# A two-block transformer kernel: order inside the attention slots, where softmax steps end, two-block dilated slots, start and end of the program

## Chip, cores and metric

The kernel runs on one core of a Trainium2 chip. The metric is device time in microseconds (us), the median of several runs. Engines are called as the profile calls them: PE (TensorE matmul; PEld its weight loads), DVE (VectorE), ACT (ScalarE), POOL (GpSimd), SP (SyncE, which issues DMAs).

## What is computed

A residual stream of 512 tokens with 1024 channels goes through a forgetting attention ("fox", 16 heads of 64), a gated linear layer, a dilated attention (8 heads, three groups of keys), a second gated layer, and then a second block: a short convolution beside an attention with a compressed, a selected and a windowed branch, and a feed-forward layer. Cut to the parts that the change touches:

```python
# fox: every head, causal, with decay c
s = q @ k.T * 64**-0.5 + c[t] - c[s]; s = where(causal, s, -inf)
o = softmax(s) @ v;  out = (o * silu(z)) @ w_out
# dilated: 8 heads, groups g = 0, 1, 2 (window 128, 512, 2048; stride 1, 4, 16)
o_g, lse_g = window_attention(q_g, k_g, v_g, slopes_g)
o = sum_g softmax(lse)_g * o_g;  out = (o * silu(z)) @ w_out
# second block, 8 heads in 2 groups
o_c = softmax(q @ k_cmp.T) @ v_cmp      # 31 compressed keys
out = gate_c * o_c + gate_s * o_sel + gate_w * o_win
```

## The kernel before

Activations lie with channels on the partitions and the 512 tokens in the free dimension. Every big product is exact to nearly fp32 by three matmuls: weights and activations are split into a high part (`hi`, written by ACT) and a rest (`lo`, subtracted by DVE), and `mm3` (lines 144 to 146) runs hi·hi, hi·lo and lo·hi with 512 columns each. `Weights` brings the weights in units of 128x1024 through SP's queue (`wraw`), makes `whi` on ACT (line 74) and `wlo` on DVE (line 85); `pump` first finishes the last `wlo`, then starts new DMAs, then the next `whi`. `plan` is the list of units in the order of their use.

The program is written out by hand; each engine runs its instructions strictly in the order in which the Python code issues them. Projections are cut into chunks of four k-steps (12 matmuls of `mm3`): `t_unit` makes two chunks of one unit and lets its last chunk evacuate the accumulator (PSUM tag `acc`, 3 banks). `weave(chunks, slots)` deals the attention's slots evenly behind the chunks.

**Fox slots.** A head has three parts (`BLOCKS`: query block 3; blocks 2 and 0; block 1), so 48 steps for 16 heads. Slot j holds `soft_end` for what is open, then `t_step(j-4)` (transposes of the probabilities into a bank `t`, 2 banks, and their copies to `pt` by ACT), then `s_step(j)`, then in every sixth slot `pv_step` (probabilities times values, one pair of heads). `s_step` takes a bank `s` (2 banks), runs the scores (lines 678, 679), adds the mask by a matmul of a bf16 identity with the mask (line 542), and starts the softmax: `soft` (line 624, DVE) adds the decay, writes `pr` and the row's extreme `st`, then ACT takes the exponential with its sum (line 628). `soft_end` finishes all open softmax steps on DVE: reciprocals of the sums (line 637), then the scaling of `pr` (lines 640, 642). It is called at the head of every slot and, in a chunk, just ahead of the evacuation. One pair of heads is a cycle of six chunks (q, k, z) and six slots; cycles 1 to 6 are alike.

**Dilated slots.** A head has 4 steps of one query block each. `s_step(h, i)` runs one score matmul of the full array (line 814) and eight with 32 columns of the array each (line 818); three DVE operations, a reduction and the exponential follow. Slots lag by 3 steps; four slots go with the 14 chunks of a head (its z first, then q and k of the next head).

**Second block.** Its 48 steps work like fox's (`mwin` as mask on DVE, no mask matmul) and are woven with the convolution's and the gates' chunks; `c_scores`, `c_soft`, `ct_step` hold the compressed branch, whose values `vc2` (64x128) are multiplied by two matmuls of 32 rows and 64 columns of the array for every pair of heads (line 1281).

Of the kernel before, what the change touches and what calls it, by code (L numbers as in the profile page):

```python
# [26 lines left out]
class Weights:  # L27
# [20 lines left out]
    def start_halves(self, n, half):  # L48

        c = slice(half * S, half * S + S)  # L50
        for i in range(n):
            if half == 0:
                self.raw[i] = self.pool.tile([P, D], F32, name="wraw", tag="wraw", bufs=self.raw_bufs)
            self.nc.sync.dma_start(self.raw[i][:, c], self.units[i][1][:, c])
        self.n_dma = n

    def prep_half(self, i, half):
# [4 lines left out]
        self.nc.scalar.activation(hi[:, c], self.raw[i][:, c], AF.Copy)  # L62
# [65 lines left out]
class Net:  # L128
# [19 lines left out]
    def t_unit(self, tag, pair, kts, evac, m=P, tag_ps="acc"):  # L148
# [7 lines left out]
        for u, lst in enumerate(kts):  # L156
            for c0 in range(0, len(lst), 4):
                sub = lst[c0 : c0 + 4]

                def chunk(u=u, sub=sub, c0=c0, first=(c0 == 0), pos=pos):  # L160
                    if pos == 0:
                        st["acc"] = self.bank(tag_ps)
                    if first:
                        st["w"] = self.w.pop(tag)
                    self.w.pump()
# [17 lines left out]
    def k_outer(self, tags, evacs, pair):  # L183
# [3 lines left out]
        def chunk(k):  # L187
            if k == 0:
                st["w"] = [self.w.pop(t) for t in tags]
                st["a"] = [self.acc() for _ in tags]  # L190
            self.w.pump()
# [35 lines left out]
    def n_chunk(self, tag, lhs, pair, evac, banks=("acc", "acc", "acc", "s")):  # L227
# [3 lines left out]
        for u in range(4):  # L231
            for half in range(2):

                def chunk(u=u, half=half):
                    if half == 0:
                        if u == 0:
                            st["a"] = [self.bank(x) for x in banks]
                        st["w"] = self.w.pop(tag)
                    if u < 3:
# [105 lines left out]
    def plan(self):  # L345
# [15 lines left out]
        for h in range(8):  # L361
# [4 lines left out]
            add("dz", "dil_z", [h])  # L366
            if h < 7:
                for g in range(3):
                    add("dq", "dil_q", [8 * g + h + 1]); add("dk", "dil_k", [8 * g + h + 1])
        add("do", "dil_o", range(8))  # L370
# [17 lines left out]
    def run(self):  # L388
# [16 lines left out]
        nc.sync.dma_start(self.gains[:, 0:5, :], t["gains"])  # L405
# [31 lines left out]
    def fox(self):  # L437
# [6 lines left out]
        warm = at.tile([P, D], BF16, name="cb", tag="cb", bufs=3)[:, :S]  # L444
        nc.vector.memset(warm, 0.0)
        nc.scalar.activation(warm[:, 0:1], warm[:, 0:1], AF.Copy)
        idle = self.bank("o")
        for _ in range(9):
            nc.tensor.matmul(idle, warm[:, :P], warm, start=True, stop=True)
        x_load = lambda k: nc.sync.dma_start(xs[:, k, :], self.rows(t["xT"], k))  # L450
        x_load(0)
        self.w.start_halves(3, 0)
        x_load(1)
        x_load(2)
        self.w.start_halves(3, 1)
        for k in range(3, KT):
            x_load(k)
        feed = lambda k: self.feed(A, k, xs[:, k, :], self.gains[:, 0, k : k + 1])
        feed(0)
        for i in range(3):  # L460
# [70 lines left out]
        def s_step(j):  # L531
            h, part = divmod(j, 3)
            p = h // 2
            if part == 0 and h + 2 < 16:
                load_c(h + 2)
            sp = self.bank("s")
            pr = at.tile([P, S], F32, name="pr", tag="pr", bufs=6)
            blocks = self.BLOCKS[part]
            for qb, c0 in blocks:
                n = (qb + 1) * P  # L540
                self.scores(sp[:, c0 : c0 + n], qs[p], ks[p], h % 2, qb, False)
                nc.tensor.matmul(sp[:, c0 + n - P : c0 + n], identb, maskb, start=False, stop=True, skip_group_check=True)
            for qb, c0 in blocks:
# [13 lines left out]
        def slot(j):  # L557
            self.soft_end()
            if 0 <= j - LAG < 48:
                self.t_step(at, pts, probs, j - LAG)  # L560
            if j < 48:
                s_step(j)
            u = j - LAG - 7
            if u >= 0 and u % 6 == 0 and u // 6 < 8:
                pv_step(u // 6)
# [107 lines left out]
    def scores(self, out, qs, ks, j, qb, stop):  # L673
# [4 lines left out]
        self.nc.tensor.matmul(out, qs[j][:, c], hi[:, 0:n], start=True, stop=False, skip_group_check=True)  # L678
        self.nc.tensor.matmul(out, qs[j][:, c], lo[:, 0:n], start=False, stop=stop, skip_group_check=True)  # L679

    def t_step(self, at, pts, probs, j):
# [6 lines left out]
        for kb in ((0,), (1, 3), (2,))[part]:  # L688
# [78 lines left out]
    def dil(self):  # L767
# [9 lines left out]
        def ev_q(h, g):  # L777
            def f(a):
                q = qs[h, g] = at.tile([P, S], F32, name="dqk", tag="dqk", bufs=10)
# [4 lines left out]
        def ev_k(h, g):  # L784
            def f(a):
                k = ks[h, g] = at.tile([P, S], F32, name="dqk", tag="dqk", bufs=10)
# [22 lines left out]
        def s_step(h, i):  # L809
            sp = self.bank("s")  # L810
            pr = at.tile([P, S], F32, name="pr", tag="pr", bufs=4)
            q, k = [qs[h, g] for g in range(3)], [ks[h, g] for g in range(3)]
            lo = 0 if i else P
# [776 lines left out]
```

## Time and profile before

| | us |
|---|---|
| median of 3 runs | 1729.88 |
| lowest, highest | 1728.58, 1729.96 |
| profiled execution, device time | 1729.0 |
| its span, first to last instruction | 1727.2 |
| PE busy | 1714.4 (99%) |
| DVE busy | 966.0 (56%) |
| ACT busy | 672.2 (39%) |
| POOL busy | 111.0 (6%) |

Busy time of PE is from a start to a modelled end, and successive matmuls overlap, so PE at 99% says that it nearly always has one in flight, not that none is late. How far one start lies behind the one before is read from the timeline. Times of rows count from the span's start. The granted TensorE clock is full in the whole span.

### The profile page before, as it was taken

How to read it: one execution, taken by the hardware profiler on the slowest of the kernel's cores; microseconds unless marked ns; L12 is line 12 of the kernel's file. 1: busy time of each engine (PE TensorE's matmuls, PEld its weight loads, DVE VectorE, ACT ScalarE, POOL GpSimd, SP SyncE). 2: the span in 40 equal slices, each digit the busy share in tenths (PEclk: the TensorE clock that was granted, in tenths of full speed). 3: DMA queues.
4: the chain of work that ended last, by engine and by line, in shares of the span. 5: the costliest groups of instructions: out<-in, count | busy, mean ns of one | idle time of the engine just before them, and what ended most of it. 6: DMA issues, size and time to landing. Idle time of an engine off the chain costs nothing.

```text
span 1727.2 us, 21619 instructions
## 1 busy us (share of the span) xinstructions
PE 1714.4 (99%) x8512; PEld 1398.8 (81%) x8512; DVE 966.0 (56%) x1692; ACT 672.2 (39%) x1146; POOL 111.0 (6%) x88
## 2 busy tenths in 40 slices
PE   8999999999999999999999999999999999999999
PEld 6777777888978888978878887777788888888887
DVE  5577774453354543354555687776554675566432
ACT  6466663522222222222235545555432333333320
POOL 2000000100000000000000421000000222111000
PEclk9999999999999999999999999999999999999999
DMA  5322224323221222221223332112243432223321
GB/s 187 130 85 87 90 74 138 125 96 133 86 86 61 86 73 98 86 86 63 85 98 121 134 124 85 58 53 88 83 142 112 163 119 98 89 97 104 142 96 61
DMA packets 57349, 173.74 MB, mean 101 GB/s; under 512 B 7440, under 2 KB 7952, under 8 KB 57248
## 3 DMA queue, kind: packets, MB, share of 16 engines
q1 hardware_dynamic: 57248, 172.36, 29.0%
q8 instruction: 67, 1.10, 0.3%
q14 instruction: 34, 0.28, 0.1%
HBM read 161.82 MB, written 10.52 MB: 100 GB/s over the span
## 4 chain that ended last, share of the span: by engine, by line
PE 96%; DVE 2%; ACT 1%; DMA 0%; issue 0%; SPq 0%; ACTq 0%; DVEq 0%
PE acc L144 22%; PE acc L145 21%; PE acc L146 21%; PE acc L248 3%; PE acc L250 3%; PE acc L249 3%; PE o L700 2%; PE t L692 2%; PE s L144 1%; PE s L145 1%; PE s L146 1%; PE s L249 1%; PE s L248 1%; PE s L679 1%; PE s L250 1%; PE s L678 1%
## 5 line engine op out<-in xcount | busy, mean ns | idle before, releaser
L85 DVE TENSOR_TENSOR wlo<-wraw,whi 128x1024 fp32r<-128x1024 f32 x267 | 347.9, 1309 | 140.1 <-ACT whi L74 140.0
L74 ACT ACTIVATE whi<-wraw 128x1024 fp32r<-128x1024 f32 x267 | 279.0, 1050 | 152.7 <-PE acc L145 64.4
L628 ACT ACTIVATE pr<-pr,st 128x512 f32<-128x512 f32 (+3 forms) x160 | 93.6, 586 | 153.4 <-DVE st L825 84.1
L291 POOL TENSOR_TENSOR nacc<-nacc,sq 128x512 f32<-128x512 f32 x35 | 47.9, 1377 | 1186.3 <-ACT sq L290 1185.9
L781 DVE TENSOR_TENSOR dqk<-acc,nacc 128x512 f32<-128x512 f32 x24 | 26.1, 1102 | 61.6 <-PE s L814 57.5
L695 ACT ACTIVATE pt<-t 128x512 f32<-128x512 f32 (+3 forms) x128 | 51.0, 424 | 21.1 <-PE t L692 20.6
L1425 ACT ACTIVATE fy<-fcv,fcw 128x512 f32<-128x512 f32 x22 | 17.9, 816 | 100.0 <-DVE fcv L1420 100.0
L1438 POOL TENSOR_TENSOR act<-fs,fu 128x512 f32<-128x512 f32 x22 | 43.2, 1966 | 191.0 <-DVE fu L1437 174.0
L692 PE MATMUL t<-ident,pr 128*128 128x128 f32 x320 | 50.8, 273 | 2.0 <-ACT pt L695 1.1
L692 PEld LDWEIGHTS t<-ident,pr 128*128 128x128 f32 x320 | 40.0, 140 | 14.0 <-DVE pr L640 1.4
L144 PE MATMUL acc<-a0h,whi 128*128 128x512 f32 x112 | 47.3, 422 | 2.0 <-ACT whi L62 1.4
L824 DVE SCALAR_TENSOR_TENSOR pr<-dist,s 128x128 f32<-128x128 f32 (+1 forms) x96 | 24.9, 314 | 42.2 <-PE s L818 42.2
L144 PE MATMUL acc<-b4h,whi 128*128 128x512 f32 x113 | 45.6, 404 | 0.0
L637 DVE RECIPROCAL st<-st 128x1 f32<-128x1 f32 x160 | 23.8, 158 | 38.6 <-ACT pr L628 38.6
L144 PE MATMUL acc<-b7h,whi 128*128 128x512 f32 x113 | 44.2, 391 | 0.0
L144 PE MATMUL acc<-b5h,whi 128*128 128x512 f32 x113 | 44.2, 391 | 0.0
L146 PE MATMUL acc<-a0h,wlo 128*128 128x512 f32 x112 | 44.1, 394 | 0.0
L144 PE MATMUL acc<-b6h,whi 128*128 128x512 f32 x113 | 44.1, 390 | 0.0
L146 PE MATMUL acc<-b7h,wlo 128*128 128x512 f32 x113 | 44.1, 390 | 0.0
L145 PE MATMUL acc<-b4l,whi 128*128 128x512 f32 x113 | 44.0, 390 | 0.0
L146 PE MATMUL acc<-b6h,wlo 128*128 128x512 f32 x113 | 44.0, 390 | 0.0
L146 PE MATMUL acc<-b4h,wlo 128*128 128x512 f32 x113 | 44.0, 389 | 0.0
(1108 smaller groups left out, 4680.7 us busy)
## 6 DMA issues: line engine op xcount, KB each, us to landing
wraw<-in_dil_q SPq DMA_DIRECT2D x24, 512.0 KB, 3.2
wraw<-in_dil_k SPq DMA_DIRECT2D x24, 512.0 KB, 3.2
wraw<-in_dil_v SPq DMA_DIRECT2D x24, 512.0 KB, 3.3
wraw<-in_f_g SPq DMA_DIRECT2D x22, 512.0 KB, 3.5
wraw<-in_f_u SPq DMA_DIRECT2D x22, 512.0 KB, 3.5
wraw<-in_f_o SPq DMA_DIRECT2D x22, 512.0 KB, 3.5
wraw<-in_gate SPq DMA_DIRECT2D x16, 512.0 KB, 3.3
wraw<-in_b_gm SPq DMA_DIRECT2D x16, 512.0 KB, 3.5
```

What stands on the lines that cost most here:

```text
L74: nc.scalar.activation(hi, t, AF.Copy)
L85: self.nc.vector.tensor_tensor(lo, t, hi.bitcast(F32), ALU.subtract)
L144: mm(acc, wh, xh, start=start, stop=False)
L145: mm(acc, wh, xl, start=False, stop=False)
L146: mm(acc, wl, xh, start=False, stop=stop)
L248: self.nc.tensor.matmul(a, sh, mh, start=(k == 0), stop=False)
L249: self.nc.tensor.matmul(a, sh, ml, start=False, stop=False)
L250: self.nc.tensor.matmul(a, sl, mh, start=False, stop=(k == KT - 1))
L291: nc.gpsimd.tensor_tensor(self.nacc[i], self.nacc[i], sq, ALU.add)
L628: self.nc.scalar.activation(pr, pr, AF.Exp, scale=-1.0, bias=st[:, 0:1], accum_out=st[:, 1:2])
L692: nc.tensor.transpose(tp[:, c : c + P], pr[:, c0 + kb * P : c0 + (kb + 1) * P], self.ident)
L695: nc.scalar.activation(pts[h][:, self.KOFF[kb] : self.KOFF[kb] + b - a], tp[:, a:b], AF.Copy)
```

## The change

- In every chunk of a projection (`t_unit`, `k_outer`, `n_chunk`, `t_two`) a call of `soft_end` stands directly ahead of `self.w.pump()`.
- A fox slot is ordered `pv_step`, `t_step`, mask matmuls, scores, softmax. In the second block `pv_step` moves to the front and the compressed branch's steps go ahead of `s_step`.
- `t_step` transposes key block 2 first, then 1 and 3, then 0.
- A dilated slot takes two query blocks: their full-array scores, then all their 32-column scores, then both softmax starts; it lags by two slots, and two slots go with a head's chunks. z is computed behind q and k of the next head, and z of heads 6 and 7 together in the last phase.
- `vc2` becomes block diagonal (64x2x128), and one matmul takes the place of two.
- At the start, the first halves of the first three weight units are issued from ACT's queue, `gains` follow the pool's set-up, and the first `whi` half is made by DVE. At the end, the last output tile is added and stored in two halves.

```diff
@@ -54 +54 @@
-            self.nc.sync.dma_start(self.raw[i][:, c], self.units[i][1][:, c])
+            (self.nc.sync if half else self.nc.scalar).dma_start(self.raw[i][:, c], self.units[i][1][:, c])
@@ -62 +62,4 @@
-        self.nc.scalar.activation(hi[:, c], self.raw[i][:, c], AF.Copy)
+        if i + half:
+            self.nc.scalar.activation(hi[:, c], self.raw[i][:, c], AF.Copy)
+        else:
+            self.nc.vector.tensor_copy(hi[:, c], self.raw[i][:, c])
@@ -164,0 +168 @@
+                    self.soft_end()
@@ -190,0 +195 @@
+            self.soft_end()
@@ -238,0 +244 @@
+                    self.soft_end()
@@ -366 +371,0 @@
-            add("dz", "dil_z", [h])
@@ -369,0 +375,2 @@
+            if h != 6:
+                add("dz", "dil_z", [h] if h < 6 else [6, 7])
@@ -405 +411,0 @@
-        nc.sync.dma_start(self.gains[:, 0:5, :], t["gains"])
@@ -444,6 +449,0 @@
-        warm = at.tile([P, D], BF16, name="cb", tag="cb", bufs=3)[:, :S]
-        nc.vector.memset(warm, 0.0)
-        nc.scalar.activation(warm[:, 0:1], warm[:, 0:1], AF.Copy)
-        idle = self.bank("o")
-        for _ in range(9):
-            nc.tensor.matmul(idle, warm[:, :P], warm, start=True, stop=True)
@@ -450,0 +451 @@
+        nc.sync.dma_start(self.gains[:, 0:5, :], t["gains"])
@@ -454,0 +456,6 @@
+        warm = at.tile([P, D], BF16, name="cb", tag="cb", bufs=3)[:, :S]
+        nc.vector.memset(warm, 0.0)
+        nc.scalar.activation(self.sel[:, 0:1], self.ones, AF.Copy)
+        idle = self.bank("o")
+        for _ in range(9):
+            nc.tensor.matmul(idle, warm[:, :P], warm, start=True, stop=True)
@@ -458,0 +466 @@
+        self.w.prep_half(0, 0)
@@ -460 +468 @@
-        for i in range(3):
+        for i in range(1, 3):
@@ -536,2 +543,0 @@
-            sp = self.bank("s")
-            pr = at.tile([P, S], F32, name="pr", tag="pr", bufs=6)
@@ -539 +545,2 @@
-            for qb, c0 in blocks:
+            sp = self.bank("s")
+            for i, (qb, c0) in enumerate(blocks):
@@ -541,3 +548,13 @@
-                self.scores(sp[:, c0 : c0 + n], qs[p], ks[p], h % 2, qb, False)
-                nc.tensor.matmul(sp[:, c0 + n - P : c0 + n], identb, maskb, start=False, stop=True, skip_group_check=True)
-            for qb, c0 in blocks:
+                nc.tensor.matmul(sp[:, c0 + n - P : c0 + n], identb, maskb, start=(i == 0), stop=False, skip_group_check=True)
+            return lambda: s_scores(h, part, sp)
+
+        def s_scores(h, part, sp):
+            p = h // 2
+            for qb, c0 in self.BLOCKS[part]:
+                n = (qb + 1) * P
+                self.scores(sp[:, c0 : c0 + n], qs[p], ks[p], h % 2, qb, True, False)
+            return lambda: s_soft(h, part, sp)
+
+        def s_soft(h, part, sp):
+            pr = at.tile([P, S], F32, name="pr", tag="pr", bufs=6)
+            for qb, c0 in self.BLOCKS[part]:
@@ -559,4 +575,0 @@
-            if 0 <= j - LAG < 48:
-                self.t_step(at, pts, probs, j - LAG)
-            if j < 48:
-                s_step(j)
@@ -565,0 +579,4 @@
+            if 0 <= j - LAG < 48:
+                self.t_step(at, pts, probs, j - LAG)
+            if j < 48:
+                s_step(j)()()
@@ -673 +690 @@
-    def scores(self, out, qs, ks, j, qb, stop):
+    def scores(self, out, qs, ks, j, qb, stop, start=True):
@@ -678 +695 @@
-        self.nc.tensor.matmul(out, qs[j][:, c], hi[:, 0:n], start=True, stop=False, skip_group_check=True)
+        self.nc.tensor.matmul(out, qs[j][:, c], hi[:, 0:n], start=start, stop=False, skip_group_check=True)
@@ -688 +705 @@
-        for kb in ((0,), (1, 3), (2,))[part]:
+        for kb in ((2,), (1, 3), (0,))[part]:
@@ -779 +796 @@
-                q = qs[h, g] = at.tile([P, S], F32, name="dqk", tag="dqk", bufs=10)
+                q = qs[h, g] = at.tile([P, S], F32, name="dqk", tag="dqk", bufs=12)
@@ -786 +803 @@
-                k = ks[h, g] = at.tile([P, S], F32, name="dqk", tag="dqk", bufs=10)
+                k = ks[h, g] = at.tile([P, S], F32, name="dqk", tag="dqk", bufs=12)
@@ -809,3 +826,2 @@
-        def s_step(h, i):
-            sp = self.bank("s")
-            pr = at.tile([P, S], F32, name="pr", tag="pr", bufs=4)
+        def s_step(h, i0):
+
@@ -812,0 +829,16 @@
+            sps = []
+            for i in (i0, i0 + 1):
+                sps.append(self.bank("s"))
+                lo = 0 if i else P
+                nc.tensor.matmul(sps[-1][:, lo:256], q[0][:, i * P : (i + 1) * P], k[0][:, (i - 1) * P + lo : (i + 1) * P],
+                                 start=True, stop=True, skip_group_check=True)
+            for i, sp in zip((i0, i0 + 1), sps):
+                for g in (1, 2):
+                    for r in range(4):
+                        nc.tensor.matmul(sp[32 * r : 32 * r + 32, 128 + g * P : 256 + g * P],
+                                         q[g][:, i * P + 32 * r : i * P + 32 * r + 32], k[g][:, r * P : (r + 1) * P],
+                                         start=True, stop=True, skip_group_check=True)
+            for i, sp in zip((i0, i0 + 1), sps):
+                s_soft(h, i, sp)
+
+        def s_soft(h, i, sp):
@@ -814,7 +846 @@
-            nc.tensor.matmul(sp[:, lo:256], q[0][:, i * P : (i + 1) * P], k[0][:, (i - 1) * P + lo : (i + 1) * P],
-                             start=True, stop=True, skip_group_check=True)
-            for g in (1, 2):
-                for r in range(4):
-                    nc.tensor.matmul(sp[32 * r : 32 * r + 32, 128 + g * P : 256 + g * P],
-                                     q[g][:, i * P + 32 * r : i * P + 32 * r + 32], k[g][:, r * P : (r + 1) * P],
-                                     start=True, stop=True, skip_group_check=True)
+            pr = at.tile([P, S], F32, name="pr", tag="pr", bufs=6)
@@ -857,2 +882,0 @@
-        LAG = 3
-
@@ -863,7 +887,8 @@
-                u = j - LAG
-                if u >= 4 and u % 4 == 0:
-                    pv_step(h0 + u // 4 - 1)
-                if 0 <= u < 16:
-                    t_step(h0 + u // 4, u % 4)
-                if j < 16:
-                    s_step(h0 + j // 4, j % 4)
+                u = j - 2
+                if u >= 2 and u % 2 == 0:
+                    pv_step(h0 + u // 2 - 1)
+                if 0 <= u < 8:
+                    for i in range(2):
+                        t_step(h0 + u // 2, u % 2 * 2 + i)
+                if j < 8:
+                    s_step(h0 + j // 2, j % 2 * 2)
@@ -871 +896 @@
-            return [lambda j=j: slot(j) for j in range(16 + LAG + 1)]
+            return [lambda j=j: slot(j) for j in range(11)]
@@ -898 +923 @@
-            ch = T("dz", ev_z(h))
+            ch = []
@@ -902,5 +927,6 @@
-            n = 4 if h < 7 else 2
-            if h == 7:
-                run(ch)
-            weave(ch if h < 7 else [], todo[:n])
-            todo = todo[n:]
+            if h < 6:
+                ch += T("dz", ev_z(h))
+            elif h == 7:
+                ch = T("dz", ev_z(6)) + T("dz", ev_z(7))
+            weave(ch, todo[:2])
+            todo = todo[2:]
@@ -964 +990,2 @@
-        vc2 = at.tile([64, P], F32, name="vc2")
+        vc2 = at.tile([64, 2, P], F32, name="vc2")
+        nc.gpsimd.memset(vc2, 0.0)
@@ -1133 +1160,4 @@
-            nc.scalar.activation(vc2, p[:, :P], AF.Copy)
+            src = p[:, :P].rearrange("p (g d) -> p g d", g=2)
+            for j in range(2):
+                r = slice(32 * j, 32 * j + 32)
+                nc.scalar.activation(vc2[r, :, 64 * j : 64 * j + 64], src[r], AF.Copy)
@@ -1280,3 +1310 @@
-                for jj in range(2):
-                    nc.tensor.matmul(ob[p][64 * jj : 64 * jj + 64, :], vc2[32 * jj : 32 * jj + 32, g * 64 : g * 64 + 64],
-                                     ptc[p][32 * jj : 32 * jj + 32, :], start=True, stop=False, skip_group_check=True)
+                nc.tensor.matmul(ob[p], vc2[:, g, :], ptc[p], start=True, stop=False, skip_group_check=True)
@@ -1291,0 +1320,3 @@
+            u = j - LAG - 7
+            if u >= 0 and u % 6 == 0 and u // 6 < 8:
+                pv_step(u // 6)
@@ -1296,0 +1328,5 @@
+            if j in (1, 19):
+                c_scores(j // 19)
+            for g in range(2):
+                if 0 <= j - 3 - 18 * g < 4:
+                    c_soft(g, j - 3 - 18 * g)
@@ -1299,8 +1334,0 @@
-                if j in (1, 19):
-                    c_scores(j // 19)
-                for g in range(2):
-                    if 0 <= j - 3 - 18 * g < 4:
-                        c_soft(g, j - 3 - 18 * g)
-            u -= 7
-            if u >= 0 and u % 6 == 0 and u // 6 < 8:
-                pv_step(u // 6)
@@ -1384,0 +1413 @@
+            self.soft_end()
@@ -1473,2 +1502,3 @@
-            v.tensor_tensor(res[n], res[n], acc[n], ALU.add)
-            nc.sync.dma_start(self.rows(t["out"], n), res[n])
+            for c in (slice(0, 256), slice(256, S)) if n == KT - 1 else (slice(0, S),):
+                v.tensor_tensor(res[n][:, c], res[n][:, c], acc[n][:, c], ALU.add)
+                nc.sync.dma_start(self.rows(t["out"], n)[:, c], res[n][:, c])
```

The order on DVE in cycle 1 of fox, from a part of 512 columns on (ISA: line 624 before, 641 after; the plain `st` is its read of the row's extreme). Before:

```order
L624 ISA pr,st<-s,cb 128x512
L624 ISA st 128x1
L85 TENSOR_TENSOR wlo<-wraw,whi 128x1024
L637 RECIPROCAL st<-st 128x1
L640 TENSOR_SCALAR pr<-pr,st 128x512
L485 SCALAR_TENSOR_TENSOR qf<-acc,rb 128x512
```

After:

```order
L641 ISA pr,st<-s,cb 128x512
L641 ISA st 128x1
L654 RECIPROCAL st<-st 128x1
L657 TENSOR_SCALAR pr<-pr,st 128x512
L88 TENSOR_TENSOR wlo<-wraw,whi 128x1024
L493 SCALAR_TENSOR_TENSOR qf<-acc,rb 128x512
```

The subtraction for the weights moved from between the softmax start and its reciprocal to behind both. The same holds at the other two places of a cycle where `wlo` stands.

The order on PE in one fox slot with two query blocks, before:

```order
L692 MATMUL t<-ident,pr 128x128 x4
L678 MATMUL s<-kk,qs 128x384
L679 MATMUL s<-b7h,qs 128x384
L542 LDWEIGHTS identb
L542 MATMUL s<-maskb,identb 128x128
L678 MATMUL s<-kk,qs 128x128
L679 MATMUL s<-b7h,qs 128x128
```

After:

```order
L709 MATMUL t<-ident,pr 128x128 x2
L548 LDWEIGHTS identb
L548 MATMUL s<-maskb,identb 128x128
L548 LDWEIGHTS identb
L548 MATMUL s<-maskb,identb 128x128
L695 MATMUL s<-kk,qs 128x384
```

The mask matmuls moved from behind each score to ahead of all, and this slot has two transposes where it had four (the slot ahead has four for two).

The order on PE at a dilated slot, before (one query block):

```order
L146 MATMUL acc<-b7h,wlo 128x512
L835 MATMUL t<-ident,pr 128x128 x4
L814 MATMUL s<-dqk 128x128
L818 MATMUL s<-dqk 32x128 x8
L144 MATMUL acc<-b0h,whi 128x512
```

After (two query blocks):

```order
L149 MATMUL acc<-b7h,wlo 128x512
L861 MATMUL t<-ident,pr 128x128 x8
L833 MATMUL s<-dqk 128x256 x2
L838 MATMUL s<-dqk 32x128 x16
L147 MATMUL acc<-b0h,whi 128x512
```

PE goes over to the 32-column form and back once for two blocks, where it went once for each.

## Rows read from the trace of the kernel before

**Rows 1.** The page's busy times: engine, us, share of the span, instructions.

```profile
PE 1714.4 (99%) x8512; PEld 1398.8 (81%) x8512; DVE 966.0 (56%) x1692; ACT 672.2 (39%) x1146; POOL 111.0 (6%) x88
```

**Rows 2.** Windows, one fox cycle: length; PE, PEld, DVE, ACT, POOL busy; clock; DMA.

```profile
134.95:159.67 24.72, 24.72 (x135) 19.08 (x134) 18.69 (x48) 15.44 (x35) 0.00 (x0) 1.00 0.25 86
```

**Rows 3.** DVE's waits in that cycle: for whom, us in total, times, longest.

```profile
DVE st L637 <- ACT pr L628: 2.1, 3, 0.9
DVE b1l L328 <- ACT b1h L327: 0.7, 1, 0.7
...
DVE pr L624 <- PE s L542: 0.5, 1, 0.5
DVE qf L485 <- PE acc L146: 0.4, 1, 0.4
```

**Rows 4.** Timeline, DVE in fox: start, us, operation, [idle before <- releaser].

```profile
151.14 0.08 DVE L624 DVE_READ_ACCUMULATOR2_ANT st<- 128x1 f32 x1
152.12 0.16 DVE L637 RECIPROCAL st<-st 128x1 f32<-128x1 f32 x1 [0.90 <-ACT pr L628]
152.50 0.16 DVE L637 RECIPROCAL st<-st 128x1 f32<-128x1 f32 x1 [0.22 <-ACT pr L628]
...
153.45 1.22 DVE L85 TENSOR_TENSOR wlo<-wraw,whi 128x1024 fp32r<-128x1024 f32 x1
...
161.00 0.16 DVE L637 RECIPROCAL st<-st 128x1 f32<-128x1 f32 x1 [0.94 <-ACT pr L628]
...
251.61 0.17 DVE L637 RECIPROCAL st<-st 128x1 f32<-128x1 f32 x1 [0.73 <-ACT pr L628]
```

**Rows 5.** Timeline, ACT in the same cycle, between two exponentials.

```profile
152.38 1.04 ACT L74 ACTIVATE whi<-wraw 128x1024 fp32r<-128x1024 f32 x1
153.33 0.63 ACT L695 ACTIVATE pt<-t 128x384 f32<-128x384 f32 x2
```

**Rows 6.** Timeline, PE: the last score of the slot whose extreme DVE reads at 151.14.

```profile
148.38 0.27 PE L679 MATMUL s<-b7h,qs 128*128 128x128 f32 x1
```

**Rows 7.** Timeline, PE's weight loads in a fox slot with two query blocks.

```profile
109.43 0.19 PEld L678 LDWEIGHTS s<-kk,qs 128*128 128x128 f32 x1
109.54 0.19 PEld L679 LDWEIGHTS s<-b7l,qs 128*128 128x128 f32 x1
109.88 0.10 PEld L542 LDWEIGHTS <-identb 128*128 128x128 bf16 x1 [0.15 <-issue]
...
110.01 0.19 PEld L679 LDWEIGHTS s<-b7l,qs 128*128 128x128 f32 x1
```

**Rows 8.** Timeline, PE at a dilated slot without transposes.

```profile
492.72 0.59 PE L814 MATMUL s<-dqk 128*128 128x256 f32 x2
493.24 0.64 PE L818 MATMUL s<-dqk 128*32 128x128 f32 x16
493.82 0.50 PE L144 MATMUL acc<-b4h,whi 128*128 128x512 f32 x1
```

**Rows 9.** Windows, the end of the dilated attention (columns as in rows 2).

```profile
860.00:900.00 40.00, 37.51 (x244) 29.39 (x243) 20.93 (x45) 13.54 (x26) 0.00 (x0) 1.00 0.25 85
```

**Rows 10.** DVE's waits in the second block's slots, 1075 to 1160 us.

```profile
DVE st L637 <- ACT pr L628: 7.8, 15, 1.2
DVE pr L624 <- PE s L679: 3.0, 2, 2.1
```

**Rows 11.** The same, 1160 to 1256 us.

```profile
DVE st L637 <- ACT pr L628: 13.0, 19, 1.4
DVE gth L1198 <- PE acc L146: 6.8, 5, 2.6
...
DVE pr L624 <- PE s L679: 6.0, 8, 2.2
```

**Rows 12.** Timeline, PE at the start; DVE's last addition.

```profile
8.10 0.50 PE L144 MATMUL acc<-a0h,whi 128*128 128x512 f32 x1 [1.44 <-ACT whi L62]
...
1723.65 0.69 DVE L1473 TENSOR_TENSOR fr<-fr,acc 128x512 f32<-128x512 f32 x1 [2.71 <-PE acc L146]
```

More of the change, by code (lines that the diff above doesn't have):

```diff
@@ L535, in s_step @@
                 load_c(h + 2)
+            blocks = self.BLOCKS[part]
             sp = self.bank("s")
-            pr = at.tile([P, S], F32, name="pr", tag="pr", bufs=6)
-            blocks = self.BLOCKS[part]
-            for qb, c0 in blocks:
-                n = (qb + 1) * P
-                self.scores(sp[:, c0 : c0 + n], qs[p], ks[p], h % 2, qb, False)
-                nc.tensor.matmul(sp[:, c0 + n - P : c0 + n], identb, maskb, start=False, stop=True, skip_group_check=True)
-            for qb, c0 in blocks:
+            for i, (qb, c0) in enumerate(blocks):
[5 more added lines that the diff above has]
+            for qb, c0 in self.BLOCKS[part]:
+                n = (qb + 1) * P
+                self.scores(sp[:, c0 : c0 + n], qs[p], ks[p], h % 2, qb, True, False)
+            return lambda: s_soft(h, part, sp)
+        def s_soft(h, part, sp):
+            pr = at.tile([P, S], F32, name="pr", tag="pr", bufs=6)
+            for qb, c0 in self.BLOCKS[part]:
                 n = (qb + 1) * P
@@ L561, in slot @@
             if j < 48:
-                s_step(j)
-            u = j - LAG - 7
-            if u >= 0 and u % 6 == 0 and u // 6 < 8:
-                pv_step(u // 6)
+                s_step(j)()()
         def fin1():
@@ L1291, in slot @@
             self.soft_end()
+            u = j - LAG - 7
+            if u >= 0 and u % 6 == 0 and u // 6 < 8:
+                pv_step(u // 6)
             u = j - LAG
@@ L1296, in slot @@
                     ct_step(u // 12)
+            if j in (1, 19):
[3 more added lines that the diff above has]
+                    c_soft(g, j - 3 - 18 * g)
             if j < 48:
                 s_step(j)
-                if j in (1, 19):
-                    c_scores(j // 19)
-                for g in range(2):
-                    if 0 <= j - 3 - 18 * g < 4:
-                        c_soft(g, j - 3 - 18 * g)
-            u -= 7
-            if u >= 0 and u % 6 == 0 and u // 6 < 8:
-                pv_step(u // 6)
         lhs = lambda x, b: x[:, b * P : (b + 1) * P]
```

## Prediction

> **What bounds the kernel now.** The page comes first [rows 1]: PE is busy 99% of the span, DVE 56%, ACT 39%. So PE sets the time, and at first sight every matmul or weight load that the change spares on PE is gained in full. The share of DVE is a mean over stages with different loads, though. So the second view is one stage by itself, a cycle of fox: in 24.72 us PE has no gap, and DVE is busy 18.69 us, 76% [rows 2]. The third view is what DVE waits for in that cycle [rows 3]: 2.1 us for exponentials, 0.7 us four times for high parts that ACT makes (one row stands for four alike), and only 0.5 + 0.4 = 0.9 us for PE. Busy time and waits on ACT are 18.69 + 2.1 + 2.8 = 23.6 us; with the 0.9 us and 0.2 us of short gaps the cycle is full. DVE's program in its order, which no instruction leaves, is a chain of 23.8 us under PE's 24.7 us. PE is the bound here by 4% only, and whatever lengthens DVE's chain by over 0.9 us per cycle makes DVE the bound. That decides this change.
>
> **soft_end at the head of every chunk.** It adds no instruction. It puts the reciprocal directly behind the softmax start, and the reciprocal waits for ACT's exponential of the same slot. What that wait is when nothing stands between is in the rows: 0.94 us for 512 columns, 0.90 + 0.22 = 1.12 us for the slot with two query blocks, 0.73 us for 256 columns [rows 4]. Before, three of the six slots of a cycle have a `wlo` there, 1.22 us [rows 4], and one has the work of `pv_step`; they cover the wait, which is why rows 3 show 2.1 us and not six full waits. After, all six are open: 2 x (0.94 + 1.12 + 0.73) = 5.6 us, 3.5 us more. Behind the waiting reciprocal stand the scaling, `wlo`, the evacuation and the next softmax start, which frees a bank `s`. DVE's chain becomes 23.8 + 3.5 = 27.3 us a cycle. ACT can add to it: after an exponential it runs `whi`, 1.04 us, and the copies of transposes, up to 0.63 us [rows 5], and DVE may reach the next softmax start sooner than ACT is done with both. I take 0.1 us for that, 27.4 us, with 28.2 us as the upper end (0.45 us at two places).
>
> PE feels this late. Scores of slot j+2 need the bank that DVE frees in slot j. Two slots are 2 x 24.72 / 6 = 8.2 us of PE's time, and DVE already trails by 151.14 - 148.38 = 2.8 us [rows 4, 6], so about 5 us of lag are free, once. Fox has six such cycles: 6 x (27.4 - 24.7) - 5 = **+11 us**. Ends: +7 (27.3 and all 8.2 us free) and +18 (28.2 and 3 us free).
>
> The second block has the same steps, about 16 triples of slots in 181 us. In its first half the waits on exponentials are 7.8 us [rows 10], and 8 triples with nothing between are 8 x 2.79 = 22.3 us: 14.5 us more. DVE waited there for PE 3.0 us [rows 10] and some 2 us in small waits, so its chain passes PE's by about 10 us, of which 5 us are free lag: **+5 us**, ends 0 and +10. The second half rises by 22.3 - 13.0 = 9.3 us, under the 6.8 + 6.0 us that DVE had left waiting for PE [rows 11]: 0. `pv_step` ahead of the transposes moves its ACT and DVE work ahead of the softmax start; that is in these sums, since it then covers no wait. In the dilated slots DVE waits for PE for long stretches, and chunks are seven to a slot: 0.
>
> **Masks first.** The mask's weights are loaded only 0.34 us behind those of the long score ahead of it, after 0.15 us in which no load runs, and from the mask's load to the turn of the next score are 0.13 us [rows 7]. So a mask behind a long score costs PE about 0.13 us. Ahead of the scores it stands behind a transpose, where the next load is open for 0.11 us [rows 7] anyway; I take 0.08 us. Over 64 masks that is 3 us less for PE, ends 0 and 8 us. In the forecast this counts nothing, since PE has time to spare in fox once DVE is the bound; only where it is not is the gain real. The order of the transposes' parts and `pv_step` in front change no count on PE: 0.
>
> The page "TensorE: Matmul & The Clock Gate", table at its head, of the Trainium skill gives TensorE a window that pulls weight loads ahead of running matmuls. By it the mask's load would lie under the score, and the 3 us would be 0; rows 7 show the load of the bf16 identity open for 0.15 us, so the row decides.
>
> **Dilated slots of two blocks.** Two full-array matmul records of 256 columns, some 0.44 us at 0.11 us for 128, are followed by the 32-column ones after 0.52 us: 0.08 us to go over. The sixteen of those run four at a time at 0.11 us a group, 0.44 us, and the next full-array load comes after 0.58 us: 0.14 us. That load is open, 0.11 us more [rows 7, 8]. One change there and back costs 0.33 us; 32 blocks have 32 of them before and 16 after: 16 x 0.33 = **-5.3 us**, on PE, which is the bound there. Ends -3 and -6.
>
> The end of this attention has slots with no chunk between them: in 40 us PE is idle 2.5 us [rows 9]. z of heads 6 and 7 now stands between, so most of these waits have cover; late then is only the last head's product, as before. **-2 us**, ends 0 and -2.5.
>
> **Start, values, end.** PE waits 1.44 us for the second unit's high part [rows 12]. Three half units are now issued by ACT beside SP. ACT's issue time has no row; nothing says that the transfers land sooner by as much as they are issued sooner, nor that ACT isn't held up. Bounds by that one wait either way, -1.4 and +1.4; I take -1. The block-diagonal values spare at most one change of form per pair of heads, 4 x 0.33 = 1.3 us; I take -0.3. The last addition, 0.69 us [rows 12], in halves: the second store is half as long, -0.2 us, ends +/-0.35.
>
> The page "TensorEngine Tiling (Array Packing)", section Tiling Modes, of the Trainium skill says that a change of tiling mode drains TensorE, and lists a product over 64 rows as a mode of its own. By it the block-diagonal matmul keeps as many changes as before, and its -0.3 us would be 0. No row here shows that form.
>
> **Sum.** Against the profiled execution of 1729.0 us: +11 + 5 - 5.3 - 2 - 1 - 0.3 - 0.2 = +7.2. The median is 1729.88, 0.9 us above that execution; I put the sum on the median: **1737 us**, slower. With the terms' nearer ends the forecast's own range is 1733 to 1743.
>
> **Rivals.**
> - *DVE's chain is covered* (faster): if the waits overlap with time that DVE had to wait anyway, or ACT's exponentials come sooner than these rows, PE stays the bound, and all that PE is spared counts: -5.3 - 2 - 3 - 1.5 = -12, 1718 us. For it: PE has no gap in the cycle now, and most of DVE's time is not busy in the mean. Against it: only 0.9 us per cycle is left, and an exponential can't start before its softmax start. It decides from a chain under 24.4 us.
> - *Only fox pays* (about the same to slightly slower): the second block's lag is taken up by its second half, which has 12 us to spare, before PE feels it: +7.2 - 5 = +2.2, 1732 us. For it: the PE waits of rows 11; against: the lag arises ahead of them.
> - *ACT joins the chain* (much slower): 28.2 us a cycle with 3 us of lag, and 10 us in the second block: +18 + 10 - 8.8 = +19, 1749 us. For it: `whi` and copies stand between exponentials [rows 5]; against: ACT is idle for a third of the cycle [rows 2].
>
> **How the numbers follow.** Forecast 0.45, DVE covered 0.23, only fox 0.20, ACT joins 0.12. This kernel's measurement tells about 0.2%, 3.5 us, from no change: below 1726.4 faster, above 1733.3 slower. Faster: 0.22 of the covered case and 0.02 of the others, 0.24. Same: 0.13 of "only fox", 0.03 of the forecast and 0.01 of the covered case, 0.17. Slower: 0.59. The range must reach into the covered case, so 1717 to 1746 us.
>
> **What would show it.** In fox's cycles of the changed kernel DVE's waits on exponentials would be near 5.6 us, the cycle near 27 us, and PE would wait for DVE (releasers of scores, `st` or `pr`). A cycle of 24.4 us with PE unbroken would make the forecast wrong at its main step. In the dilated slots there must be 16 runs of 32 records in the 32-column form, with one change of form each; the end of that attention must have lost most of its idle time. First matmuls that start later than now would turn the start's term round.

## The result and the profile after

| | us |
|---|---|
| before, median of 4 runs (lowest, highest) | 1729.92 (1728.58, 1730.33) |
| after, median of 4 runs (lowest, highest) | 1744.93 (1744.47, 1746.62) |
| ratio, 95% interval | 1.0092 [1.0076, 1.0108] |
| span of the profiled execution, before, after | 1727.2, 1743.2 |

The changed kernel is 15 us slower; forecast were 7. The page's busy line of the changed kernel, to be held against [rows 1], shows nothing of it: PE is at 99%, with 6 us more of busy time, since a late or slow matmul counts as busy too.

```profile
PE 1720.5 (99%) x8504; PEld 1410.6 (81%) x8504; DVE 969.2 (56%) x1694; ACT 670.5 (38%) x1146; POOL 112.2 (6%) x89
```

Both kernels run the same 5472 matmuls of `mm3` in nearly the same order, so the start of the n-th can be compared between two traces. That gives the loss by stage, in us:

| stage, up to this matmul of mm3 | before | after | difference in the stage |
|---|---|---|---|
| start, 97th | 83.95 | 83.83 | -0.1 |
| fox, 673rd | 280.73 | 298.30 | +17.7 |
| dilated attention, 2785th | 1003.49 | 1011.57 | -9.5 |
| second block's attention, 3553rd | 1286.38 | 1301.89 | +7.4 |
| the rest, last | 1723.22 | 1738.73 | 0.0 |
| end of the span | 1727.22 | 1743.17 | +0.4 |

**Fox.** One cycle of the changed kernel by its windows (columns: length, then busy time of each engine, granted clock), then DVE's waits and PE's waits in it (total, times, longest). They answer [rows 2, 3].

```profile
core 0: us, PE busy (x) PEld busy (x) DVE busy (x) ACT busy (x) POOL busy (x), PEclk, DMA share, GB/s
150.69:178.02 27.33, 26.11 (x132) 19.77 (x133) 18.87 (x48) 15.38 (x35) 0.00 (x0) 1.00 0.25 78
```

```profile
DVE st L654 <- ACT pr L645: 5.3, 8, 1.0
DVE b6h L682 <- ACT kk L681: 0.7, 1, 0.7
...
DVE b2l L334 <- ACT b2h L333: 0.7, 1, 0.7
```

```profile
PE s L548 <- DVE st L641: 0.5, 1, 0.5
PE t L709 <- ACT pt L712: 0.4, 1, 0.4
PE o L717 <- ACT pt L712: 0.2, 1, 0.2
```

The cycle is 27.33 us, before it was 24.72. DVE's busy time is nearly what it was; its waits for exponentials have grown from 2.1 to 5.3 us, four waits of 0.7 us a cycle for ACT's high parts stand as before (the window takes in a fifth at its edge), and its waits for PE are gone. DVE's program order is the bound. DVE's timeline there shows the waits one by one, in the places of [rows 4]; the number ahead of the arrow is the idle time:

```profile
151.89 0.16 DVE L654 RECIPROCAL st<-st 128x1 f32<-128x1 f32 x1 [0.73 <-ACT pr L645]
154.02 0.17 DVE L654 RECIPROCAL st<-st 128x1 f32<-128x1 f32 x1 [0.97 <-ACT pr L645]
154.22 0.49 DVE L657 TENSOR_SCALAR pr<-pr,st 128x512 f32<-128x512 f32 x1
154.63 1.22 DVE L88 TENSOR_TENSOR wlo<-wraw,whi 128x1024 fp32r<-128x1024 f32 x1
159.27 0.08 DVE L641 DVE_READ_ACCUMULATOR2_ANT st<- 128x1 f32 x1
162.34 0.16 DVE L654 RECIPROCAL st<-st 128x1 f32<-128x1 f32 x1 [0.95 <-ACT pr L645]
```

PE's timeline has the scores to which the softmax read at 159.27 belongs:

```profile
151.79 0.27 PE L696 MATMUL s<-b7h,qs 128*128 128x128 f32 x1
```

The low part of the weights now stands behind the wait that it covered. From the start of the last score, 151.79, to the read at 159.27 it is 7.5 us of lag, where [rows 4, 6] have 151.14 - 148.38 = 2.8. At fox's end PE pays for that lag. Its timeline there and the windows around it:

```profile
256.45 0.39 PE L696 MATMUL s<-b7h,qs 128*128 128x512 f32 x1
260.02 0.44 PE L709 MATMUL t<-ident,pr 128*128 128x128 f32 x2 [3.19 <-ACT pt L712]
```

```profile
256.80:260.00 3.20, 0.04 (x1) 0.00 (x0) 1.93 (x3) 1.62 (x4) 0.00 (x0) 1.00 0.51 164
260.00:264.40 4.40, 4.29 (x15) 3.54 (x16) 2.63 (x10) 3.00 (x7) 0.00 (x0) 0.61 0.01 2
```

PE stands for 3.2 us, and behind that the granted clock is 0.61 in the mean of 4.4 us: part of the matmuls run at 1.2 instead of 2.4 GHz, so the wait costs some 1.4 us more than itself, added up over the starts of `mm3`'s matmuls there.

**Second block.** Most of its 7.4 us is lost at one place. The row of PE's timeline, the windows around it, and rows of DVE and ACT ahead of it:

```profile
1108.30 1.11 PE L709 MATMUL t<-ident,pr 128*128 128x128 f32 x4 [3.95 <-ACT pt L712]
```

```profile
1096.00:1108.50 12.50, 8.06 (x39) 6.57 (x40) 9.15 (x26) 5.89 (x15) 0.00 (x0) 0.96 0.12 36
1108.50:1114.00 5.50, 5.16 (x15) 3.99 (x15) 3.74 (x14) 3.67 (x10) 0.00 (x0) 0.50 0.04 16
```

```profile
1097.31 0.16 DVE L654 RECIPROCAL st<-st 128x1 f32<-128x1 f32 x1 [0.88 <-ACT pr L645]
...
1097.97 0.68 DVE L1288 TENSOR_REDUCE cst<-nacc 128x16 f32<-128x512 f32 x1
1098.68 0.69 DVE L1289 TENSOR_TENSOR nacc<-nacc,cst 128x512 f32<-128x512 f32 x1
1099.29 0.55 DVE L641 CUSTOM_DVE_ANT_0 pr<-s,mwin 128x384 f32<-128x384 f32 x1
```

```profile
1107.13 0.63 ACT L333 ACTIVATE b1h<-ac 128x512 fp32r<-128x512 f32 x1 [3.14 <-DVE ac L1209]
1107.66 0.58 ACT L712 ACTIVATE pt<-t 128x512 f32<-128x512 f32 x1
```

The steps of the compressed softmax (L1288, L1289) now stand ahead of the softmax start (L641). DVE comes late to `ac`, ACT waits 3.14 us for it, and the copy that frees PE's bank of transposes stands behind that in ACT's order. PE waits 3.95 us, and then runs 5.5 us at a granted clock of 0.50.

**Dilated attention.** PE's timeline of a slot of two blocks: 32 records in the 32-column form in one run, as [rows 8] had 16; the window 860:900, where [rows 9] had 37.51 us busy, is full.

```profile
518.13 1.02 PE L833 MATMUL s<-dqk 128*128 128x256 f32 x4
519.09 1.08 PE L838 MATMUL s<-dqk 128*32 128x128 f32 x32
520.10 0.50 PE L147 MATMUL acc<-b0h,whi 128*128 128x512 f32 x1
520.44 0.40 PE L148 MATMUL acc<-b0l,whi 128*128 128x512 f32 x1
```

```profile
860.00:900.00 40.00, 40.00 (x294) 33.97 (x287) 21.32 (x47) 13.95 (x27) 0.00 (x0) 1.00 0.12 40
```

### The profile page after: what moved, and what is told of

Read it like the earlier page. It is cut to its first block, busy times and chain, and to the rows that moved or that the text cites. A ratio compares the mean times of both kernels' runs of the same rounds, so it can differ in the third digit from the quotient of the medians.

```text
span 1743.2 us, 21610 instructions
## 1 busy us (share of the span) xinstructions
PE 1720.5 (99%) x8504; PEld 1410.6 (81%) x8504; DVE 969.2 (56%) x1694; ACT 670.5 (38%) x1146; POOL 112.2 (6%) x89
## 4 chain that ended last, share of the span: by engine, by line
PE 82%; DVE 10%; ACT 6%; issue 1%; DMA 0%; ACTq 0%; DVEq 0%; SPq 0%
PE acc L147 18%; PE acc L149 18%; PE acc L148 18%; PE acc L254 3%; PE acc L256 3%; PE acc L255 3%; ACT pr L645 3%; DVE wlo L88 2%; ACT whi L77 1%; PE s L149 1%; PE s L148 1%; PE s L147 1%; DVE pr L641 1%; PE s L255 1%; PE s L254 1%
## 5 line engine op out<-in xcount | busy, mean ns | idle before, releaser
L712 ACT ACTIVATE pt<-t 128x256 f32<-128x256 f32 (+3 forms) x128 | 50.6, 422 | 13.0 <-PE t L709 12.9
L148 PE MATMUL acc<-a0l,whi 128*128 128x512 f32 x112 | 44.1, 394 | 0.3 <-DVE a0l L337 0.3
L147 PE MATMUL acc<-a1h,whi 128*128 128x512 f32 x112 | 44.3, 395 | 0.0
```

The lines of the kernel that those rows point to most:

```text
L147: mm(acc, wh, xh, start=start, stop=False)
L148: mm(acc, wh, xl, start=False, stop=False)
L712: nc.scalar.activation(pts[h][:, self.KOFF[kb] : self.KOFF[kb] + b - a], tp[:, a:b], AF.Copy)
```

## The experiments

All were run in five rounds beside the kernel before; each set shares its runs of before (median 1730.05 for the first four, 1730.23 for the next, 1728.67 for the last). "Stage" means the difference to before between the matmuls of the table above, in the profiled execution.

In the diffs of e1 to e4 one of the four places of the call stands for all; e5 and e7 show what they add to e1, e10 what it adds to e8.

**e1: the calls at the heads of chunks taken out.**

```diff
-                    self.soft_end()
                     self.w.pump()
```

> The changed kernel without the four soft_end calls at the heads of chunks; all else of the change stays. Theory 1 (VectorE stands in its program order at each exponential, and that alone makes fox and the second block longer): fox gives back its 17.7 us and the second block its 7.4 us, so 1718 to 1721 us, 9 to 12 us under the kernel before; the fox cycle is 24.4 to 24.7 us and VectorE's waits for exponentials in it fall from 5.3 to about 2 us. Rival 1 (the new order inside a slot, products and transposes ahead of the scores, is what makes the cycle longer): the cycle stays above 26 us and the time at 1738 us or more.

Measured: 1722.12 us, ratio 0.9957 [0.9945, 0.9970]. Fox is 2.5 us shorter than before, its cycle 24.49 us; DVE's waits for exponentials in one, 134:158.4:

```profile
DVE st L651 <- ACT pr L642: 2.5, 4, 0.9
```

The calls make fox's loss: 17.7 + 2.5 = 20.2 us. But the second block still loses 5.1 us, so its 7.4 us are not the calls' alone.

**e2: only the calls, in the kernel before.**

```diff
+                    self.soft_end()
                     self.w.pump()
```

> The kernel before with nothing but the four soft_end calls at the heads of chunks. Theory 1: all of the loss and none of the gain, 1729.9 + 17.7 + 7.4 = 1755 us (1750 to 1758), fox cycle 27.2 to 27.5 us. Rival 1: the calls alone cost little, 1728 to 1734 us.

Measured: 1748.27 us, 1.0105 [1.0091, 1.0119]. Stages: fox +14.6 (cycle 26.3 us), dilated attention +0.7, second block +4.9. Faster than expected: 1755 took the losses of the whole change for those of the calls. Fox's other new orders add 1 us to a cycle, and in the second block the losses overlap. PE's waits there, 1085:1210:

```profile
PE t L695 <- ACT pt L698: 2.3, 1, 2.3
PE o L1274 <- DVE b4l L331: 1.5, 1, 1.5
```

The first is the same bank at the same place, the second another place. The calls alone cost 4.9 us, the rest alone 5.1 (e1), both together 7.4.

**e3: the calls in the first block only.**

```diff
-                    self.soft_end()
+                    if self.fox_like:
+                        self.soft_end()
```

> The changed kernel with the calls at the heads of chunks in the first block (fox, dilated attention) only, none in the second block. Theory 1: the second block gives back 7.4 us, the first keeps its cycle of 27.3 us: 1737.5 us (1736 to 1739). Rival 2 (the loss of the second block comes from the new places of the compressed softmax and of the products): 1743 to 1746 us.

Measured: 1743.39 us, 1.0078 [1.0064, 1.0092]; second block +5.1. Rival 2 holds: of the 7.4 us there 5.1 remain without the calls.

**e4: the calls one step later.**

```diff
-                    self.soft_end()
                     self.w.pump()
+                    self.soft_end()
```

> The changed kernel with the same calls moved one step, behind pump() at the head of the chunk, so that the low part of the next weights (1.22 us, three per fox cycle) stands between the softmax start and the reciprocal again. Theory 1: three of six waits are covered, 0.97 + 0.95 + 0.84 = 2.8 us less VectorE time a cycle, cycle 24.5 to 24.8 us, time 1720 to 1727 us. Rival 3 (ScalarE's chain of exponential, high part and copies sets the 27.3 us): the cycle stays within 0.5 us of 27.3 and the time within 4 us of 1745.

Measured: 1721.93 us, 0.9954 [0.9941, 0.9966], fox's cycle 24.49 us; second block +3.9. Three covered waits of a cycle decide; ACT's chain, the rival of 28.2 us a cycle, doesn't set the time.

**e5: e1 with the compressed softmax behind the scores again.**

```diff
-            if j in (1, 19):
-                c_scores(j // 19)
-            for g in range(2):
-                if 0 <= j - 3 - 18 * g < 4:
-                    c_soft(g, j - 3 - 18 * g)
             if j < 48:
                 s_step(j)
+                if j in (1, 19):
+                    c_scores(j // 19)
+                for g in range(2):
+                    if 0 <= j - 3 - 18 * g < 4:
+                        c_soft(g, j - 3 - 18 * g)
```

> As the run without heads (1722.1 us), and with the compressed scores and their softmax steps behind the slot's own scores again, as in the kernel before. In the run without heads the second block still lost 5 us in one place, 3.2 us in which TensorE waits for a bank of transposes and ten matmuls at the lower clock behind it. Theory 2 (the four steps of the compressed softmax, each 0.7 to 1.4 us on VectorE, now stand ahead of the softmax start and hold up its exponential, the copy behind that and so the bank): the 5 us are gone, 1717 us. Rival 2b (another part of the slot's new order, the parts of the transposes or the products in front, holds the bank): 1721 to 1723 us.

Measured: 1717.97 us, 0.9931 [0.9919, 0.9944]; second block +0.1. The window 1075:1125, first of the changed kernel, then of e5:

```profile
1075.00:1125.00 50.00, 45.02 (x209) 34.60 (x209) 36.93 (x93) 24.15 (x56) 2.59 (x2) 0.93 0.19 62
```

```profile
1075.00:1125.00 50.00, 48.24 (x257) 37.81 (x256) 37.08 (x106) 28.68 (x72) 2.56 (x2) 1.00 0.17 54
```

The place of the compressed branch's scores and softmax is a second cause, and the clock is full again.

**e6: the whole change with fox's `pv_step` at the slot's end.**

```diff
-            u = j - LAG - 7
-            if u >= 0 and u % 6 == 0 and u // 6 < 8:
-                pv_step(u // 6)
             if 0 <= j - LAG < 48:
                 self.t_step(at, pts, probs, j - LAG)
             if j < 48:
                 s_step(j)()()
+            u = j - LAG - 7
+            if u >= 0 and u % 6 == 0 and u // 6 < 8:
+                pv_step(u // 6)
```

> The changed kernel, all calls at the heads kept, with fox's pv_step back at the end of the slot. With the calls alone the cycle was 26.3 us, with the whole change 27.3 us. Theory 3 (pv_step's work on ScalarE and VectorE covered one of the waits for an exponential; ahead of the slot it covers none): the cycle goes back to 26.3 us and the time to 1738 to 1741 us. Rival 3b (the masks ahead of the scores or the parts of the transposes lengthen the chain): the cycle stays at 27.3 us and the time within 1.5 us of 1744.9.

Measured: 1739.84 us, 1.0060 [1.0047, 1.0072], cycle 26.29 us. `pv_step`'s cover is worth 1.0 us a cycle.

**e7: the calls in three of fox's cycles.** Set where fox weaves its cycles; the calls stand under `if self.head`.

```diff
         for p in range(1, 7):
+            self.head = p < 4
```

> The run without heads (1722.1 us), with the calls back in three of fox's six full cycles, the first three (slots 6 to 23). They lengthen a cycle by 27.3 - 24.5 = 2.8 us, 8.5 us in all. Forecast's term (some 5 us of lag between TensorE and VectorE are free, once): 1722.1 + 8.5 - 5 = 1725.6 us. Theory 4 (lag is only lent: VectorE gains 0.2 us a cycle on TensorE afterwards, and the rest is paid back at fox's last slots, which have no chunk between them): the first three cycles cost TensorE 5 to 6 us, the end of fox the rest, 1722.1 + 8.5 - 0.6 = 1730 us (1729 to 1732, with a fall of the clock).

Measured: 1730.78 us, 1.0007 [0.9998, 1.0016], 8.7 us over e1. Fox costs 6.87 + 2.47 = 9.34 us more than in e1, and three cycles are longer by 3 x (27.33 - 24.49) = 8.5 us. The cycle falls from 27.33 over 25.32 to 24.49 us, and at fox's end PE waits for the copy of a transpose, 180:290:

```profile
PE t L714 <- ACT pt L717: 2.0, 2, 1.7
```

No 5 us are free: lag that three cycles run up is paid behind them, in the next cycle and at fox's end.

**e8: calls behind `pump`, compressed softmax behind the scores, last store whole.**

> The changed kernel with three of its parts taken back: the calls stand behind pump() (1721.9 us alone), the compressed softmax behind the slot's scores, the last store in one piece. Theory 2: 1721.9 - 3.8 (what the second block still lost with the calls behind pump()) - 0.3 = 1717.8 us (1716.5 to 1719), 12 us under the kernel before. Rival 2b: 1721 to 1722 us.

Measured: 1717.50 us, 0.9929 [0.9916, 0.9943]. Stages: start +0.2, fox -2.8, dilated -9.5, second block 0.0.

**e9: the dilated part alone, in the kernel before.** The diff is that of the dilated attention in the change.

> The kernel before with the dilated part of the change alone (slots of two blocks, lag of two, 12 buffers, z of heads 6 and 7 behind head 7's slots). Theory: all of what the changed kernel gains in its dilated attention, 17.6 - 8.1 = 9.5 us between the same products of the two traces, is this part's own: 1730 - 9.5 = 1720.5 us (1720 to 1722). The forecast's terms say -7.3: 1722.7 us. If the gain were VectorE catching up after fox's loss, the part alone would gain under 5 us: over 1725 us.

Measured: 1720.99 us, 0.9953 [0.9941, 0.9966], 7.7 us under its runs of before. In the profiled execution the stage is -7.9 us, with 1.6 us of low clock in it (last section); without that -9.5, as in the changed kernel, e4, e5, e7, e8 and e12. The gain is this part's own.

**e10: e8 with fox's masks behind the scores.**

```diff
-            for i, (qb, c0) in enumerate(blocks):
-                n = (qb + 1) * P
-                nc.tensor.matmul(sp[:, c0 + n - P : c0 + n], identb, maskb, start=(i == 0), stop=False, skip_group_check=True)
...
-                self.scores(sp[:, c0 : c0 + n], qs[p], ks[p], h % 2, qb, True, False)
+                self.scores(sp[:, c0 : c0 + n], qs[p], ks[p], h % 2, qb, False)
+                nc.tensor.matmul(sp[:, c0 + n - P : c0 + n], identb, maskb, start=False, stop=True, skip_group_check=True)
```

> The best version so far (1717.5 us) with fox's masks behind their scores again. The fox cycle without waits was 24.5 us with masks first and 24.7 us in the kernel before. If the masks' place is the reason, eight cycles give back 1.5 to 2 us: 1719 to 1719.5 us. The forecast's value of the place, 0.05 us for each of 64 masks where TensorE sets the time, says 3 us: 1720.5 us. If the place costs nothing: 1717.5 us.

Measured: 1719.05 us (1716.57 to 1719.20; e8: 1716.91 to 1718.11). The ranges overlap, so the times don't settle it. The traces speak for a cost: cycles of 24.66 and 24.49 us, 0.17 for eight masks. In all of fox that is 0.7 to 1.1 us: its stage is -1.8 us in e10, and -2.5 to -2.8 in the six runs with masks first that have this cycle of 24.49 us.

**e11: e8 with the start as before.** The diff is that of the start in the change, turned round.

> The best version so far (1717.5 us) with the start as in the kernel before. In the profiled executions the start gained 1.0 us where the clock stayed at the full level and lost 0.2 us where it fell behind the 1.1 to 1.6 us in which TensorE waits for its first product. So 1717.3 to 1718.5 us; the forecast's term (-1) says 1718.5 us.

Measured: 1718.41 us (1717.14 to 1719.54), 0.9939 [0.9927, 0.9952]. Inside what the runs spread. The traces leave the start's worth open as well: up to the 97th matmul of `mm3`, the ten profiled executions with the new start lie between 1.1 us ahead of the kernel before and 0.2 us behind it, the four with the old start between 0.65 us ahead and level.

**e12: e8 with 12 warming matmuls.**

```diff
-        for _ in range(9):
+        for _ in range(12):
```

> The best version so far (1717.5 us) with 12 instead of 9 warming matmuls, so that TensorE has work until its first product (9 of them end at 5.2 us, the first product starts at 6.2 to 6.8 us). If the fall of the clock at the start comes from that idle time, it stays away and the time is 0.5 to 1.3 us lower: 1716.2 to 1717 us. If the clock falls in any case, or the first product then starts later: 1717.5 us or more.

Measured: 1715.69 us (1715.51 to 1717.37), 0.9927 [0.9915, 0.9939], the lowest median of all; but against its own runs of before e8 is as good, 0.9929, and the ranges of the two touch. Granted clock in 0:14, first the changed kernel, then e12, then e5, which has 9:

```profile
0.00:14.00 14.00, 11.15 (x32) 6.67 (x33) 7.23 (x13) 8.68 (x15) 1.81 (x6) 0.88 0.86 285
```

```profile
0.00:14.00 14.00, 11.48 (x36) 6.01 (x37) 6.64 (x12) 8.07 (x14) 1.00 (x5) 1.00 0.81 277
```

```profile
0.00:14.00 14.00, 11.39 (x37) 6.13 (x37) 7.23 (x13) 8.69 (x15) 1.81 (x6) 1.00 0.84 285
```

PE's wait for its first product is 0.6 us in place of 1.3, and the clock stays full. That the three matmuls more do it is not shown: with 9 of them the clock fell in four profiled executions (the changed kernel, e6, e7, e8) and stayed full in five (e1, e3, e4, e5, e10), and up to the 97th matmul of `mm3` e12 is only 0.2 us ahead of e8.

## Why the forecast had the sign right and half the size

Rows of DVE's and PE's timelines in fox's first cycles of the changed kernel, for the second point:

```profile
113.47 0.69 DVE L641 CUSTOM_DVE_ANT_0 pr<-s,cb 128x512 f32<-128x512 f32 x1
```

```profile
105.83 0.39 PE L696 MATMUL s<-b7l,qs 128*128 128x512 f32 x1
123.36 0.44 PE L709 MATMUL t<-ident,pr 128*128 128x128 f32 x2 [0.44 <-ACT pt L712]
```

- **The calls in fox: mechanism and cycle right.** Forecast were 5.6 us of waits for exponentials and 27.4 us a cycle; measured 5.3 and 27.33. That all six waits are open, `pv_step`'s among them, is shown by e6, and that `wlo` was the cover, by e4.
- **The step that failed is the free lag.** The term was 6 x (27.4 - 24.7) - 5 = +11; measured +17.7, and 6 x (27.33 - 24.72) = 15.7 already without what was subtracted. The 5 us were read from one steady cycle, as if they never had to be given back. In the changed kernel the lag is used up early: in the first of the six cycles the softmax start at 113.47 us comes 7.6 us behind the start of its last score (5.1 us in the kernel before), and PE waits from 123 us on, in the second. By the starts of `mm3`'s matmuls against the kernel before, PE loses 0.5 us in the first cycle, 2.6 us in each of the five others, and 5.4 us more in the stretch behind them: fox's last slots hand the lag back, 3.2 us in one wait and some 1.4 us at the low clock behind it. (Ahead of these cycles and behind this stretch it gains 1.2 us, which makes +17.7.) e7 shows the handing back by itself. The upper end, +18, comes near by luck: it stood for ACT's cycle of 28.2 us, which is not there.
- **Second block: +5 forecast, +7.4 measured, the place misjudged.** The calls alone do cost 4.9 us there (e2), but at two places, with waits of 2.3 and 1.5 us, not over eight triples. The prediction priced `pv_step`'s move and left out that of the compressed softmax, four steps of DVE ahead of softmax starts, which costs 5.1 us by itself (e1, e5). The two overlap. Of the 4.9 us some 1.6, and of the 5.1 some 2.2, is the fall of the clock, which no term held (added up over the starts of `mm3`'s matmuls at 427 instead of 227 ns).
- **Dilated attention: -5.3 - 2 forecast, -9.5 measured.** The idle 2.5 us of [rows 9] are gone but for a wait of 0.2 us. The change of form is worth what was forecast: from the first score to the next product it was 493.82 - 492.72 = 1.10 us for one block [rows 8] and is 520.10 - 518.13 = 1.97 us for two, and the second product starts 0.34 us behind the first instead of 0.23, now once for two blocks. So a pair saves 2.20 - 1.97 + 0.11 = 0.34 us, where 0.33 was forecast. Together that is 2.3 + 16 x 0.34 = 7.7 us; where the other 1.8 us come from was not tried.
- **Masks first: 0 where DVE is the bound, 3 us where PE is.** Measured in the second case: 0.7 to 1.1 us (e10, by the traces), about a third. The Trainium skill's page "TensorE: Matmul & The Clock Gate", table at its head, has loads pulled ahead of running matmuls, which makes it 0. The cycles of 24.66 and 24.49 us speak for a cost, but a smaller one than [rows 7] were read to say.
- **Start -1, values -0.3, end -0.2.** Measured -0.1, no gain and +0.4. The start's first product comes 1.1 us later and the clock falls behind the wait; what is won by 84 us just makes up for it. What the start is worth by itself stays open (e11). The second block of e8 is 0.0 us from before, with the block-diagonal product in it, and PE's timeline has it alone: from the first of these matmuls to the next product it is 1.00 us in the kernel before (1109.03 to 1110.03) and 1.05 us in e8 (1096.18 to 1097.23). The Trainium skill's page "TensorEngine Tiling (Array Packing)", section Tiling Modes, lists a product over 64 rows as a configuration of its own, and has a change of mode drain TensorE; by that no change of mode is spared, and the trace agrees: nothing is gained. From the last product's start to the end of the span it is 4.1 to 4.5 us with the store in halves and 4.0 to 4.2 with it whole.

The sum again with measured terms: -0.1 + 17.7 - 9.5 + 7.4 + 0.4 = +15.9; the spans differ by 16.0. *DVE's chain is covered* is out for the change as it stands and came true where cover was given back (e4: 1721.9, forecast 1718; of the difference 3.9 us are the second block's). *Only fox pays* is out: the second half of the second block took nothing back. *ACT joins the chain* named 1749 us, nearer than the forecast, but by a cycle that isn't there.

## What to carry to other kernels

An instruction that waits for another engine should have work ahead of it in its own engine's order; count the covers that a reordering takes away, one by one, as here `wlo`, `pv_step` and the compressed softmax. Lag between two engines is a loan: take it off a loss only if the stage that follows has room to give it back. Price every moved step, those of a side branch too, at the tightest place it passes, and don't add up two losses that wait at the same bank.

## What the runs showed of the hardware

A wait of PE can cost more than its length. The granted clock stood at half (0.50 of full, 1.2 instead of 2.4 GHz) behind waits of 3.95 us (second block) and in part behind 3.2 us (end of fox) and 1.3 us (start); matmuls of `mm3` then start 427 ns apart instead of 227, and added up over such starts the low stretches cost some 1.9, 1.4 and 1.6 us in the changed kernel, 4.9 together. The kernel before has the full clock throughout, also behind its wait of 1.44 us [rows 12], and e3, with the start of the changed kernel and a wait of 1.32 us there, keeps it too. No waiting is needed, either: behind 16 matmuls with one column each, the clock falls in 7 of the 14 profiled executions, so in e9 and not in e12. PE's timeline of both:

```profile
371.26 2.81 PE L303 MATMUL o<-ones,nacc 128*128 128x1 f32 x16
...
375.00 0.63 PE L144 MATMUL acc<-b7h,whi 128*128 128x512 f32 x1
375.43 0.63 PE L145 MATMUL acc<-b7l,whi 128*128 128x512 f32 x1
```

```profile
368.69 2.81 PE L309 MATMUL o<-ones,nacc 128*128 128x1 f32 x16
...
372.14 0.40 PE L147 MATMUL acc<-b7h,whi 128*128 128x512 f32 x1
372.38 0.39 PE L148 MATMUL acc<-b7l,whi 128*128 128x512 f32 x1
```

That is 1.3 to 1.6 us of difference between executions with the same work at that place; what decides which of them falls is open.
